# Hybrid decoder layer, one core: attention constants moved to the right of SBUF and closed with attention, and a third buffer for the raw gate and up weights

## The chip, the cores and the metric

One Trainium2 chip; the kernel runs on one of its cores. The metric is the device time of one execution in microseconds (us), as a median over runs. A core has TensorE (matrix products; PE in the profile, with its weight loads as PEld), VectorE (DVE), ScalarE (ACT), GpSimd (POOL) and SyncE, whose queue (SP) issues every DMA of this kernel. SBUF is the on-chip memory of 128 partitions, PSUM the memory that products are summed in.

## What is computed

One decoder layer on x of 1024 tokens by 1024 channels, all in float32:

```
n   = rms_norm(x)
h   = x + [ DiffAttn(n) || GLA(n) ] @ w_out
m   = rms_norm(h)
out = h + (silu(m @ w_ffn_gate) * (m @ w_ffn_up)) @ w_ffn_down
```

DiffAttn has 4 heads with two softmax maps each, GLA 4 heads of gated linear attention in chunks. The hidden width of the last line is 2816.

## The kernel before

**Precision.** Float32 products are made of three passes: each operand is cut into a high part (a cast on ScalarE, line 251) and a low part (a subtraction on VectorE, line 252), and `mm3` (lines 260 to 262) issues three matmuls per product. A cut of a weight block therefore needs the raw block in SBUF, then ScalarE, then VectorE, and only then TensorE.

**Stages.** (1) Projection of n, with both attentions woven into it by a planner (`Order`). (2) Out-projection: `po` products, h, its squares and a copy scaled by the gain (`Bf`). (3) Gate and up products, in 11 pairs (`pr` 0 to 10) of 256 hidden columns. (4) The down product.

**Gate and up.** Each pair has m = 0 (gate) and m = 1 (up). One level of a Strassen scheme makes seven products per m out of four quarters of the 1 MB raw weight block `fr`. In the trace a pair runs B11, B21, T1, T2, B22, T3, T4 (so named after the activation side), each for m = 0 and then m = 1, twelve matmuls each. The weight side is made by `a_operands` (lines 1022 to 1049): cuts a to g, of which a, b and g read the raw block, and the sums S1 to S4, made by VectorE in pair 0 and by GpSimd in all others. The high and low parts sit in rings of four (`uh`, `ul`), the sums in a ring of four (`sf`). So cut a of a pair needs the ring place of cut f of the pair before, and S1 of a pair the place of its predecessor's S4.

`load_gu(pr + 1)` stands at the top of pair `pr` and issues two loads of 1 MB, m = 0 and m = 1, into a ring of two buffers. A buffer is free again when cut g, the last reader of the raw block, is done (`ugl` in the trace).

**Activation side, pair 0 only.** `b_operands` makes T1 to T4 from h, four subtractions and four cuts each, on ScalarE and VectorE between the products. h's normalization (`rstd_begin`, `rstd_end`, lines 894 to 907) and the silu of pair 0 (`first_rest`, lines 1074 to 1090) are put into pair 0 and 1 as well.

**Order.** In this stage nothing fixes the order of an engine's instructions by hand: the framework's scheduler places each one as early as its inputs and its buffer allow, taking the one that stands first in the program where several are ready. Each engine, and the SP queue, then executes its list strictly in order. The first projection block and the end of the last pair with the down product (`tail`) keep the compute engines in program order.

**SBUF.** Pools are stacks, one from the left and one from the right. A tile in a reused place waits for the last accesses of the tiles that lay there. Left: `keep`, `const`, `small`, `ntp` (64 KB per partition: the four activation tiles, first of n, at last `mT`), `wp`, then others over it, `fl` (T2 to T4) among them; after `ntctx.close()` the pools `da` and `dw` of the down product begin behind `keep`. Right: `edge`, then `sp`, `ep`, `dp` of attention, and after `actx.close()` in their place `bp`, `fw` (with `fr`) and `fq`, and last `dl`. By the shapes, `const` and `small` take about 12.4 KB per partition, the ten `ar` buffers of `da`, into which the activations A come back, 20 KB, one `fr` buffer 8 KB.

Of the kernel before, what the change touches and what calls it, by code (L numbers as in the profile page):

```python
# [9 lines left out]
F32 = mybir.dt.float32  # L10
# [8 lines left out]
P = 128  # L19
# [3 lines left out]
ND = D // P  # L23
# [14 lines left out]
EDGE = 24  # L38
# [121 lines left out]
def decoder_layer(ctx: ExitStack, tc, xt, vecs, lams, w_proj, w_up, w_gu, w_dn, out):  # L160
    nc = tc.nc

    def pool(name, bufs=1, side="left", **k):
        return tc.tile_pool(name=name, bufs=bufs, side=side, reuse_waits="tile", **k)

    keep = ctx.enter_context(pool("keep"))
    ntctx = ExitStack()
    const = ntctx.enter_context(pool("const"))
    small = ntctx.enter_context(pool("small", 3))
    ntp = ntctx.enter_context(pool("ntp"))  # L170
    psum = ctx.enter_context(tc.tile_pool(name="psum", bufs=2, space=PSUM))
    dram = ctx.enter_context(tc.tile_pool(name="dram", bufs=1, space=DRAM))
# [14 lines left out]
    ndist = keep.tile([P, T], F32, name="ndist")  # L187


    vec = const.tile([P, 24], F32, name="vec")  # L190
    ones = const.tile([P, P], F32, name="ones")

    rsx = const.tile([P, NT], F32, name="rsx")
    nlam = const.tile([P, 1], F32, name="nlam")
# [78 lines left out]
    mixed_d = [[dram.tile([P, 512], F32, name=f"mixed{hf}_{c}") for c in range(ND)] for hf in range(2)]  # L273


    wctx, actx = ExitStack(), ExitStack()

    ctx.enter_context(pool("edge", 1, "right")).tile([P, EDGE], F32, name="edge")
    wp = wctx.enter_context(pool("wp"))
    sp = actx.enter_context(pool("sp", 1, "right"))  # L280
    ep = actx.enter_context(pool("ep", 4, "right"))
# [599 lines left out]

    def load_gu(pr):
        for m in range(2):
            raw = fw.tile([P, ND, 256], F32, name=f"fr{pr}_{m}", tag="fr", bufs=2)
            nc.sync.dma_start(raw, w_gu[pr, m].rearrange("p (d j) -> p d j", j=256))
            raws[pr, m] = raw

# [42 lines left out]
    for k, (o, n) in enumerate(OUT_COLS):  # L930
        b = NIN + k
        left = list(range(ND)) if k + 1 < len(OUT_COLS) else []
        for hf in range(2):
            if k == 0 and hf == 1:
# [4 lines left out]
                fw = fctx.enter_context(pool("fw", 1, "right"))  # L939
# [21 lines left out]
            if k == 2:  # L961
                if hf == 0:
                    load_gu(0)
                mT[hf] = new_nt(hf, "f")
                if hf == 0:
                    for c in range(ND):
                        split_b(0, c)

                    for d in range(4):
                        minus(Bf[0], Bf[2], Bf[0], d)  # L970
                    for d in range(2):
                        minus(Bf[2], Bf[3], Bf[2], d)
# [120 lines left out]
    for pr in range(NJ // 2):  # L1093
        if pr + 1 < NJ // 2:
            load_gu(pr + 1)
# [294 lines left out]
```

## Time and profile before

| | |
|---|---|
| median of 3 runs | 1244.76 us (1244.07 to 1244.89) |
| the profiled execution, its own time | 1243.45 us |
| its span, first to last instruction | 1241.7 us |
| TensorE busy | 1200.0 us, 97% |
| VectorE, ScalarE, GpSimd busy | 71%, 46%, 23% |
| mean granted TensorE clock | 0.995 |

All times below are from the span's start. A matmul's row is its modelled duration; the distance from one start to the next is what it costs when they follow each other without a gap.

### The profile page before, as it was taken

To read this page: it belongs to the slowest core of one execution; us is meant where nothing else is said; L and a number is where in the kernel's file an instruction comes from. 1 tells how busy PE (TensorE), PEld (TensorE's weight loads), DVE (VectorE), ACT (ScalarE), POOL (GpSimd) and SP (SyncE) were. 2 spreads that over 40 slices of the span, in tenths; PEclk is the share of its full clock that TensorE was granted. 3 is DMA by queue.
4 is the path that set the end of the run, shared out by engine and by line. 5 is a ranking of instruction groups with operands and counts; after the bars stand their busy time and mean duration, and the time that the engine had idled before them with its cause. 6 is when DMAs were issued, how large, how long until landed. Compare 5 with 4: busy or idle time off the path is not lost.

```text
span 1241.7 us, 17110 instructions
## 1 busy us (share of the span) xinstructions
PE 1200.0 (97%) x6068; PEld 1009.5 (81%) x6068; DVE 877.7 (71%) x1804; ACT 574.3 (46%) x1171; POOL 281.3 (23%) x282
## 2 busy tenths in 40 slices
PE   7899998999889999999989999999999999999998
PEld 7789888889878977788768788888888888888787
DVE  6765489854888777536997576866678656667885
ACT  6656354555544666635643333333333335443432
POOL 5500414000431000000053444534345330000000
PEclk9999999999999999999999999999999999999999
DMA  6101010101100623221023231322223268753351
GB/s 214 44 22 53 8 52 18 52 26 61 39 31 20 193 78 120 86 93 69 1 102 152 69 113 74 127 100 96 103 85 127 89 250 303 257 153 93 94 178 69
DMA packets 57656, 121.41 MB, mean 98 GB/s; under 512 B 5969, under 2 KB 25570, under 8 KB 53346
## 3 DMA queue, kind: packets, MB, share of 16 engines
q1 hardware_dynamic: 57570, 120.31, 28.6%
q8 instruction: 48, 0.79, 0.3%
q14 instruction: 38, 0.31, 0.1%
HBM read 88.04 MB, written 32.24 MB: 97 GB/s over the span
## 4 chain that ended last, share of the span: by engine, by line
PE 79%; DVE 11%; ACT 3%; DMA 3%; issue 2%; POOL 1%; SPq 0%; DVEq 0%; ACTq 0%; POOLq 0%
PE X L262 6%; PE X L260 6%; PE X L261 6%; PE pp L260 5%; PE pp L262 5%; PE pp L261 5%; PE s L411 3%; PE Z L262 3%; PE Z L261 3%; PE Z L260 3%; PE po L455 2%; PE po L260 2%; PE po L262 2%; PE po L261 2%; PE V L262 2%
## 5 line engine op out<-in xcount | busy, mean ns | idle before, releaser
L260 PE MATMUL pp<-wh,nh 128*128 128x384 f32 (+1 forms) x512 | 184.1, 360 | 9.4 <-ACT wh L256 7.2
L261 PE MATMUL pp<-wl,nh 128*128 128x384 f32 (+1 forms) x512 | 176.3, 344 | 0.7 <-DVE wl L257 0.7
L262 PE MATMUL pp<-wh,nl 128*128 128x384 f32 (+1 forms) x512 | 176.5, 345 | 0.0
L260 PEld LDWEIGHTS pp<-wh,nh 128*128 128x128 f32 x512 | 97.7, 191 | 18.6 <-ACT wh L256 7.2
L261 PEld LDWEIGHTS pp<-wl,nh 128*128 128x128 f32 x512 | 97.6, 191 | 2.8 <-DVE wl L257 1.8
L262 PEld LDWEIGHTS pp<-wh,nl 128*128 128x128 f32 x512 | 97.0, 189 | 3.0 <-issue 2.4
L1036 POOL TENSOR_TENSOR S1f<-fr 128x512 f32<-128x512 f32 x20 | 27.3, 1366 | 247.9 <-DVE ndist L907 238.0
L1130 POOL TENSOR_TENSOR ac<-ac,gt 128x512 f32<-128x512 f32 x30 | 46.4, 1547 | 159.8 <-DVE ac L1115 151.9
L1127 ACT ACTIVATE gt<-gt 128x512 f32<-128x512 f32 x40 | 25.3, 633 | 112.1 <-DVE gt L1126 58.8
L424 ACT ACTIVATE e<-e,nm 128x128 f32<-128x128 f32 (+7 forms) x64 | 49.3, 772 | 33.2 <-DVE nm L416 33.1
L260 PE MATMUL po<-mh,wh 128*128 128x512 f32 x128 | 51.2, 402 | 0.0
L262 PE MATMUL po<-mh,wl 128*128 128x512 f32 x128 | 50.6, 395 | 0.0
L261 PE MATMUL po<-ml,wh 128*128 128x512 f32 x128 | 50.4, 394 | 0.0
L257 DVE SCALAR_TENSOR_TENSOR wl<-wr,vec,wh 128x384 fp32r<-128x384 f32 (+1 forms) x64 | 39.5, 644 | 13.7 <-ACT wh L256 13.6
L1036 POOL TENSOR_TENSOR S4f<-fr,S2f 128x512 f32<-128x512 f32 x20 | 34.0, 1700 | 52.8 <-DVE ucl L252 52.1
L551 POOL TENSOR_TENSOR go<-go,gs 128x1024 f32<-128x1024 f32 x4 | 10.2, 2546 | 143.5 <-ACT gs L550 143.5
L1128 DVE TENSOR_TENSOR gt<-gt,ndist 128x512 f32<-128x512 f32 x40 | 31.6, 789 | 15.7 <-ACT gt L1127 14.0
L252 DVE TENSOR_TENSOR ufl<-S3f,ufh 128x512 fp32r<-128x512 f32 x22 | 15.2, 691 | 38.7 <-ACT ufh L251 38.7
L256 ACT ACTIVATE wh<-wr,vec 128x384 fp32r<-128x384 f32 (+1 forms) x64 | 37.1, 613 | 11.4 <-DMA wr<-in_w_proj 9.7
L416 DVE CUSTOM_DVE_ANT_0 e<-s,ndist 128x512 f32<-128x512 f32 (+3 forms) x64 | 36.7, 586 | 7.9 <-PE s L411 6.2
L455 PE MATMUL po<-v,wT 128*128 128x128 f32 x288 | 39.8, 283 | 1.7 <-ACT wT L445 1.7
L650 PE MATMUL pa<-Q,X 128*128 128x128 f32 x224 | 32.2, 290 | 9.3 <-POOL X L637 9.2
(555 smaller groups left out, 3539.3 us busy)
## 6 DMA issues: line engine op xcount, KB each, us to landing
fr<-in_w_gu SPq DMA_DIRECT2D x22, 1024.0 KB, 4.8
A<-act SPq DMA_DIRECT2D x77, 256.0 KB, 3.1
wr<-in_w_proj SPq DMA_DIRECT2D x72, 192.0 KB, 2.4
act<-ac SPq DMA_DIRECT2D x11, 1024.0 KB, 3.9
B<-in_w_dn SPq DMA_DIRECT2D x44, 256.0 KB, 5.4
act<-sm SPq DMA_DIRECT2D x11, 768.0 KB, 5.3
h<-in_xt SPq DMA_DIRECT2D x16, 256.0 KB, 4.9
hd<-h SPq DMA_DIRECT2D x16, 256.0 KB, 2.0
```

What stands on the lines that cost most here:

```text
L256: nc.scalar.activation(hi, src, AF.Copy, scale=gain)
L257: nc.vector.scalar_tensor_tensor(lo, src, gain, hi.bitcast(F32), ALU.mult, ALU.subtract)
L260: nc.tensor.matmul(ps, ah, bh, start=first, stop=False, **k)
L261: nc.tensor.matmul(ps, ah, bl, start=False, stop=False, **k)
L262: nc.tensor.matmul(ps, al, bh, start=False, stop=last, **k)
L411: nc.tensor.matmul(ps[m][:, :n], self.qk["q", hq][a][r, P * iq : P * iq + P], self.qk["k", ch][b][r, :n], start=(j == 0), stop=(j == 2))
L416: nc.vector.tensor_tensor_reduce(e[m][:, 512 * ch : 512 * ch + n], ps[m][:, :n], ndist[:, o : o + n], scale=-slope, scalar=nm[:, m, 0:1] i ...
L424: nc.scalar.activation(e[m][:, :cols], e[m][:, :cols], AF.Exp, bias=nm[:, m, nch - 1 : nch], scale=-1.0, accum_out=l[:, m : m + 1])
L455: nc.tensor.matmul(po[:, 0:P], self.wT[i, g][:, P * k : P * k + P], self.v[g][:, k, :], start=(kb == 0), stop=(kb == i))
L650: nc.tensor.matmul(pa[:, k], X[:, lv, :], Q[:, lv], start=True, stop=True)
L1036: (eng.tensor_sub if op == "-" else eng.tensor_add)(r, a, b)
L1130: nc.gpsimd.tensor_mul(quarter(q), quarter(q), g)
```

## The change

The constants and the small tiles go from the left stack to the right one, below the attention pools, and are closed with them; `vec` and `ones`, which later stages read, move into `keep` (`vec` is widened from 24 to 32 columns). The ring `fr` has three buffers instead of two. No arithmetic, no transfer and no line of the engines' work is added or removed.

```diff
     keep = ctx.enter_context(pool("keep"))
-    ntctx = ExitStack()
-    const = ntctx.enter_context(pool("const"))
-    small = ntctx.enter_context(pool("small", 3))
+    ntctx, wctx, actx = ExitStack(), ExitStack(), ExitStack()
+
+    ctx.enter_context(pool("edge", 1, "right")).tile([P, EDGE], F32, name="edge")
+    const = actx.enter_context(pool("const", 1, "right"))
+    small = actx.enter_context(pool("small", 3, "right"))
     ntp = ntctx.enter_context(pool("ntp"))
...
-    vec = const.tile([P, 24], F32, name="vec")
-    ones = const.tile([P, P], F32, name="ones")
+    vec = keep.tile([P, 32], F32, name="vec")
+    ones = keep.tile([P, P], F32, name="ones")
...
-    wctx, actx = ExitStack(), ExitStack()
-
-    ctx.enter_context(pool("edge", 1, "right")).tile([P, EDGE], F32, name="edge")
     wp = wctx.enter_context(pool("wp"))
     sp = actx.enter_context(pool("sp", 1, "right"))
...
-            raw = fw.tile([P, ND, 256], F32, name=f"fr{pr}_{m}", tag="fr", bufs=2)
+            raw = fw.tile([P, ND, 256], F32, name=f"fr{pr}_{m}", tag="fr", bufs=3)
```

## Rows read from the trace of the kernel before

**Rows 1.** Waits of TensorE from 600 to 1020 us: total, times, longest.
```profile
PE X L262 <- DVE ual L252: 3.5, 2, 2.0
PE X L260 <- ACT uah L251: 0.9, 1, 0.9
```

**Rows 2.** Busy time by stretch: start:end, length, each engine, granted clock, DMA.
```profile
600.00:640.00 40.00, 36.39 (x145) 27.84 (x144) 39.42 (x54) 21.08 (x35) 8.41 (x5) 0.96 0.14 53
640.00:700.00 60.00, 60.00 (x259) 48.28 (x258) 42.94 (x53) 21.49 (x38) 25.64 (x16) 1.00 0.27 99
...
636.00:638.00 2.00, 2.00 (x7) 1.52 (x6) 2.00 (x4) 0.61 (x2) 0.00 (x0) 0.50 0.00 0
```

**Rows 3.** Timeline of TensorE, pair 0 into pair 1: start, us, instruction.
```profile
621.11 0.40 PE L260 MATMUL X<-T4h,ugh 128*128 128x512 f32 x1
...
621.59 0.40 PE L262 MATMUL X<-T4h,ugl 128*128 128x512 f32 x1
...
626.47 0.39 PE L262 MATMUL X<-T4h,ugl 128*128 128x512 f32 x1
...
629.20 0.50 PE L262 MATMUL X<-fh,ual 128*128 128x512 f32 x1 [1.54 <-DVE ual L252]
...
634.25 0.50 PE L262 MATMUL X<-fh,ual 128*128 128x512 f32 x1 [2.00 <-DVE ual L252]
...
637.54 0.63 PE L260 MATMUL Y<-fh,ubh 128*128 128x512 f32 x1
...
639.39 0.40 PE L262 MATMUL Y<-fh,ubl 128*128 128x512 f32 x1
```

**Rows 4.** Timeline of the SP queue in the same stretch.
```profile
515.48 1.23 SPq L885 DMA_DIRECT2D fr<-in_w_gu  x2
...
621.37 1.62 SPq L885 DMA_DIRECT2D fr<-in_w_gu  x2
```

**Rows 5.** Timeline of ScalarE: the two cuts a of pair 1.
```profile
626.26 0.62 ACT L251 CAST uah<-fr 128x512 fp32r<-128x512 f32 x1 [1.56 <-DMA fr<-in_w_gu]
...
629.76 0.60 ACT L251 CAST uah<-fr 128x512 fp32r<-128x512 f32 x1
```

**Rows 6.** Timeline of VectorE, pair 0 into pair 1.
```profile
607.59 0.68 DVE L252 TENSOR_TENSOR uel<-S4f,ueh 128x512 fp32r<-128x512 f32 x1
...
615.81 0.69 DVE L1115 TENSOR_TENSOR ac<-Z,u 128x512 f32<-128x512 f32 x1 [0.32 <-PE Z L262]
...
620.62 0.68 DVE L252 TENSOR_TENSOR ugl<-fr,ugh 128x512 fp32r<-128x512 f32 x1
...
627.39 1.76 DVE L252 TENSOR_TENSOR ual<-fr,uah 128x512 fp32r<-128x512 f32 x1
...
632.44 1.75 DVE L252 TENSOR_TENSOR ual<-fr,uah 128x512 fp32r<-128x512 f32 x1
...
638.68 0.68 DVE L252 TENSOR_TENSOR ucl<-S1f,uch 128x512 fp32r<-128x512 f32 x1
...
652.25 1.28 DVE L252 TENSOR_TENSOR uel<-S4f,ueh 128x512 fp32r<-128x512 f32 x2
```

**Rows 7.** Timeline of GpSimd: its first sum of the stage.
```profile
626.43 2.17 POOL L1036 TENSOR_TENSOR S1f<-fr 128x512 f32<-128x512 f32 x1 [238.03 <-DVE ndist L907]
```

**Rows 8.** Costliest groups, GpSimd's S1: busy, mean ns of one, idle before.
```profile
L1036 POOL TENSOR_TENSOR S1f<-fr 128x512 f32<-128x512 f32 x20 | 27.3, 1366 | 247.9 <-DVE ndist L907 238.0
```

**Rows 9.** Timelines of ScalarE and TensorE, start of pair 3.
```profile
708.52 0.62 ACT L251 CAST uah<-fr 128x512 fp32r<-128x512 f32 x1 [1.33 <-DMA fr<-in_w_gu]
...
709.26 0.47 PE L260 MATMUL X<-T4h,ugh 128*128 128x512 f32 x1 [0.87 <-ACT uah L251]
```

**Rows 10.** Timelines of SP, TensorE and ScalarE, last pair into the down product.
```profile
996.74 0.32 SPq L1224 DMA_DIRECT2D A<-act  x1
...
1013.29 0.40 PE L260 MATMUL X<-T3h,ufh 128*128 128x512 f32 x1
...
1027.40 0.62 ACT L251 CAST da_5h<-A 128x512 fp32r<-128x512 f32 x1
```

## The prediction

> **What bounds the kernel now.** I read the page's engine totals first: TensorE is busy for 1200.0 of 1241.7 us, so only its gaps and its clock can give time back. The list of its waits says which gaps the raw gate and up weights cause: in the whole stage two waits for `ual`, the low half of cut a, 3.5 us together, and one for `uah`, its high half, 0.9 us [rows 1]. The table by stretch says where: from 600 to 640 us TensorE is busy 36.39 of 40 with a clock of 0.96, while the next 60 us are full at 1.00 [rows 2]. In those 40 us VectorE is busy for 39.42: it has nothing left to give.
>
> The timeline of TensorE gives the price of that place. A matmul follows the one before after 0.233 us (621.11 to 626.47 is 23 steps). From the last matmul of T4 at 626.47 to the first of B21 at 637.54 there are 25 steps (24 matmuls of B11 lie between), which make 5.82 us without a gap and took 11.07: 5.25 lost. From 637.54 to 639.39 five steps took 1.85 instead of 1.16: 0.69 more. Together 5.94 us [rows 3]. The two waits are 3.54 of it. Most of the other 2.4 us came behind them, when the granted clock from 636 to 638 us was 0.50, that is 1.2 in place of 2.4 GHz [rows 2]; the two gaps stand directly ahead of that fall.
>
> What ends last there: both loads of pair 1 are issued at 621.37 [rows 4], when cut g of pair 0 frees the buffer (`ugl` at 620.62, [rows 6]). The first block is there 4.9 us later, at 626.26, where ScalarE's cut has waited for the DMA [rows 5]; TensorE was through with T4 at 626.7. Then VectorE is late: `ual` starts at 627.39 and 632.44, in its strict order among the silu work of pair 0, and takes 1.76 instead of the 0.68 of `ugl`, because GpSimd's sums run beside it [rows 6, 7]. Pair 3 repeats this in small: a block comes late, TensorE idles for 0.87 us [rows 9].
>
> **The change part by part.**
>
> *The third buffer.* Pair 1's m = 0 block gets a buffer that nobody in the stage has used, so its load can follow the two of pair 0 at 515.48 [rows 4] and be done some 90 us before its use. From then on m = 0 is loaded a pair ahead, and m = 1 goes into the buffer that cut g of m = 0 frees, so it arrives when m = 0 did before. Issues and bytes are the same.
>
> Cut a of m = 0 can then be made as soon as its ring place is free, when the first half of T3 of pair 0 ends (ahead of 621.11), and stands in VectorE's list directly behind `ugl`. The block of m = 1 is there at 626.3 as before; TensorE needs its low half at the third matmul, 626.7 + 14 x 0.233 = 630.0, and VectorE reaches it at about 626.25 + 0.6 (the first `ual`) + 1.2 (one multiply) = 628.1. So both waits of [rows 1], and the clock's fall behind them, can go: 5.94, with pair 3's 0.87 a gain of 6.8 us at most.
>
> *What is late next.* VectorE: its work from 607 to 653 us is the same, and it is full. Two things eat into the gain.
>
> First, GpSimd moves. S1 of pair 1, m = 0, finds its block there and starts when its ring place is free, which is when VectorE's `uel` of pair 0 has read S4, at 608.27 [rows 6]; S2 of m = 0 follows. Before, GpSimd was idle for 238 us until 626.43 [rows 7]. Each of the two holds a VectorE subtraction up by 1.76 - 0.68 = 1.08 us [rows 6]: 2.2 us. What is queued behind them on VectorE is T3's and T4's low halves and `ugl`; for `ugl` TensorE waits, with little slack: it ends at 621.30 and its matmul starts at 621.59 [rows 3, 6]. Take off this 0.29 and the 0.32 that VectorE idled at 615.81 [rows 6]: T4 waits for 1.6 us, and the loads of `fr` behind `ugl` go out as much later. The bounds are 0, if the sums fall between two instructions, and 2.2; I take 1.6, since VectorE has no other gap there.
>
> That GpSimd and VectorE hold each other up is told by the 1.76 against 0.68. The Trainium skill says it more sharply (SBUF — State Buffer, "Who interferes with whom"): a VectorE instruction with two SBUF inputs and a GpSimd instruction that reads SBUF need the same locked port pair, and the second to come waits for the whole of the first. By that, at S1's mean of 1.37 us [rows 8], the two would cost 2.7 instead of 2.2, T4 would wait for 2.1, and the gain would be 0.5 smaller. The row decides.
>
> Second, what VectorE makes next. TensorE would be 5.94 - 1.6 = 4.3 us ahead of before, VectorE not. `ucl` was done at 639.36, its matmul came at 637.54 + 24 x 0.233 + 0.69 + 0.47 = 644.3: 4.9 us of lead, enough. `uel` was done at 652.9 [rows 6] and needed two products (48 steps) after that, at 655.5: 2.6 us of lead, 1.7 short. Bounds 0, if the scheduler puts `uel` ahead of pair 0's sums of tokens (its inputs come earlier too), and 1.7; I take 1.2, nearer to the upper end, because those sums stand first in the program.
>
> So this place gains 5.94 - 1.6 - 1.2 = 3.1 us. Pair 3 gives 0.87 more: with its two loads no longer one behind the other its block is a few us earlier.
>
> *Pairs 2 to 10.* There too S1 and S2 of m = 0 move ahead, into stretches where VectorE is busy 43 of 60 us [rows 2], and the rings of four let cuts be made several products ahead. I take 0; with that cover gone each would cost one held subtraction, 1.08 us.
>
> *The load at 517 us.* 1 MB more beside the out-projection's weights, and `fr` may start a little later, as it now lies on other attention tiles. Pair 0's products begin at 586 us (T4's start less 6 products of 5.6 and the normalization's matmuls), so 60 us cover it: 0.
>
> *The constants.* The attention stages see the same pools on fresh addresses: 0. `Bf` now lies on `const`, whose last reader is the last transpose of attention; the instructions that write `Bf` stand behind that transpose's evacuation on ScalarE: 0. At the end, `da` no longer has the 12.4 KB of `const` and `small` ahead of `mT`. Before, its 22 KB of weights and 20 KB of A ended inside the first two `mT` tiles, free after B21 of pair 10, and the first loads went out from 996.74 on. Now A buffers 5 to 9 lie on the third tile, which B22 reads until 1013.3: the load of A5 waits there, and on SP every load behind it. At the 4.9 us that 1 MB took it lands before 1018.2; its cut was at 1027.40 [rows 10]. 9 us of cover: 0.
>
> **Sum.** 3.1 + 0.9 = 4.0 us. Against the profiled execution 1243.45 - 4.0 = 1239.5 us (its span 1237.7); the median of the runs lies 1.3 above that execution, so 1240.8 us.
>
> **The rivals.** 0.2%, 2.5 us, is about what a measurement of this kernel can tell from no change.
>
> *The whole gain*, chance 0.2: the early sums fall into gaps, `uel` is made in time. 6.8 us, at least 6.3 with one short wait: 1238 to 1238.5. For it speaks that the scheduler takes each instruction as early as it can; against it the 39.42 of 40.
>
> *The wait moves*, 0.25: T4 waits 2.2 us and everything after it is paced by VectorE, whose total has not changed. What is left of the 5.94 is its 2.6 us of lead less 2.2, and pair 3's 0.87: 1.3, so 1243.5, not to be told from no change. If the third load is not issued early (the change doesn't do what it says, within the 0.25), pair 3 alone remains.
>
> *Slower*, 0.13: the gap ahead of T4 comes on top. If `ual` is still listed among the silu work, as before, T4's 2.2 us shift `ugl`, the load of m = 1 and both waits with it: 2.2 lost, 0.9 won at pair 3, and a second fall of the clock at the 2.4 us that the first cost: 1248.5. It decides once `ual` of m = 0 is not made when T4 ends.
>
> **How the numbers follow.** The forecast has 0.42, 1240.8, and its own range, 1239.5 to 1242.2, from its bounds. The range of 8 in 10 reaches down to the whole gain, 1238.0, and up past the wait that moves, 1245.2, and leaves out the slower case. Faster by over 0.2% are the forecast and the whole gain, 0.62, of which I give 0.02 to its upper edge: 0.60; within 0.2% 0.27; slower 0.13.
>
> **What would show it.** Right: a third load of `fr` near 517 us; S1 on GpSimd near 608; `ual` of m = 0 right behind `ugl`; TensorE waiting 1 to 2 us in T4 and not for `ual`; a clock of 1.00 from 626 to 642; no wait at pair 3; A5 issued when B22 ends, no cut waiting for it. Wrong: the waits for `ual` still there, a new low clock, TensorE waiting in the out-projection for weights that the early load held up, or in the down product for A.

## The result, and the profile after

The changed kernel takes 1256.13 us (median of 7 runs, 1251.66 to 1259.78), the kernel before, in runs taken beside it, 1244.89 (7 runs, 1244.07 to 1250.36): a ratio of 1.008, 95% interval 1.0062 to 1.0098. It is slower by 0.8%, some 11 us. The forecast, 1240.8 us in a range up to 1245.2, was wrong.

The profiled execution took 1259.78 us, with a span of 1258.0. Its page shows at once that no engine has more to do:

```profile
span 1258.0 us, 17115 instructions
...
PE 1208.4 (96%) x6068; PEld 1013.9 (81%) x6068; DVE 854.8 (68%) x1804; ACT 575.3 (46%) x1171; POOL 271.5 (22%) x282
```

VectorE, which was to be the limit, is busy for less time than before (68% of a longer span, against 71%). The loss is in gaps of TensorE. Its list of waits from 560 to 1060 us, the gate and up stage, answers to [rows 1]:

```profile
PE X L262 <- DVE ac L1114: 10.8, 8, 2.1
PE X L264 <- DVE ual L254: 0.7, 1, 0.7
PE Z L264 <- DVE ucl L254: 0.4, 1, 0.4
PE X L264 <- DVE ugl L254: 0.3, 1, 0.3
```

The first line is new: eight waits, 10.8 us, for an instruction that TensorE never waited for in the kernel before, `ac <- X` (line 1114 of the changed kernel, 1115 before). Here the accumulated T3 of m = 1 is read out of PSUM. T4 of m = 1 is accumulated on the same bank `X`, so its first matmul may not start before that read is done.

How much each pair lost is read from the first matmul of T4 in each pair. In the kernel before they start at 621.11, 666.23, 705.43, 745.59, 784.62, 823.66, 862.71, 901.75, 940.78, 979.83 and 1018.87 us: 39.04 a pair where nothing waits. After, they start at 627.98, 669.37, 712.35, 752.94, 793.38, 834.16, 873.36, 913.98, 954.46, 994.87 and 1035.35. This gives an account of the whole difference between the two profiled executions, 16.3 us:

| stretch | before | after | difference |
|---|---|---|---|
| start to T4 of pair 0 | 621.11 | 627.98 | +6.87 |
| T4 of pair 0 to T4 of pair 1 | 45.12 | 41.39 | -3.73 |
| T4 of pair 1 to T4 of pair 10 | 352.64 | 365.98 | +13.34 |
| T4 of pair 10 to the end | 222.8 | 222.6 | -0.2 |

**The first line belongs in the main to these two executions.** It is there before the stage begins: the two loads of `fr` that stood at 515.48 [rows 4] stand at 522.34 now, 6.86 later. Up to there VectorE, ScalarE, GpSimd and SP have the same lists of instructions in both traces, and the difference is in the clock, which in the kernel after fell, for instance, in these two stretches, where the kernel before kept 1.00:

```profile
324.00:333.00 9.00, 7.22 (x43) 7.19 (x43) 6.46 (x26) 1.31 (x2) 4.88 (x8) 0.81 0.01 2
372.00:380.00 8.00, 6.29 (x32) 6.30 (x33) 7.28 (x26) 0.43 (x2) 4.55 (x8) 0.79 0.00 0
```

(Start and end, length, busy time and instructions of TensorE, its weight loads, VectorE, ScalarE and GpSimd, granted clock, DMA share, GB/s.) The number of such falls ahead of 515 us differs from one execution to the next; the kernel with the moved pools alone (e1) has one of the two as well and takes the time of before. What sets them off stays open. The profiled execution of the changed kernel is the slowest of its seven runs, that of the kernel before is faster than all seven beside, so that the 16.3 us between them are 5 more than the 11.2 between the medians. Whether the other 2 us of this line belong to the change is not shown: T4 of pair 0 starts between 624.0 and 627.0 us in all nine experiments, later than in the one trace of the kernel before, and the fall near 326 us stands in seven of the eight traces with three buffers and in none of the three with two.

**The second line is what the change was meant to do**, 3.73 us against the 3.1 forecast. The size is less sure than it looks: with two buffers this step took 45.12 us in the kernel before and 45.13 in e6, but 43.61 in e1, so the gain lies between 2.2 and 3.7.

**The third line is the loss**, and it makes up the ratio: 13.34 - 3.73 - 0.2 = 9.4 us of some 11. Of its nine steps seven lost 1.4 to 1.7 us, one 0.2, and the first 3.9, since the clock fell behind its wait (in e2, where a wait of 2.11 us stands at this place and no fall behind it, this step takes 41.42 us in place of 42.98). The first matmuls of m = 1 of T4, with their waits, then the stretch of the fall:

```profile
674.46 0.48 PE L262 MATMUL X<-T4h,ugh 128*128 128x512 f32 x1 [2.14 <-DVE ac L1114]
...
716.61 0.47 PE L262 MATMUL X<-T4h,ugh 128*128 128x512 f32 x1 [1.31 <-DVE ac L1114]
...
757.05 0.47 PE L262 MATMUL X<-T4h,ugh 128*128 128x512 f32 x1 [1.17 <-DVE ac L1114]
...
958.53 0.48 PE L262 MATMUL X<-T4h,ugh 128*128 128x512 f32 x1 [1.11 <-DVE ac L1114]
```

```profile
674.00:678.00 4.00, 3.54 (x9) 2.88 (x10) 2.80 (x5) 0.00 (x0) 1.66 (x1) 0.60 0.01 4
```

**Why the read is late** is seen when VectorE's and GpSimd's timelines are laid side by side. First the kernel before, from pair 3 into pair 4 (VectorE, then GpSimd; start, duration):

```profile
743.70 0.68 DVE L1115 TENSOR_TENSOR gt<-X,p 128x512 f32<-128x512 f32 x1
744.41 1.23 DVE L1126 TENSOR_TENSOR gt<-gt,ndist 128x512 f32<-128x512 f32 x1
745.57 0.68 DVE L252 TENSOR_TENSOR ual<-fr,uah 128x512 fp32r<-128x512 f32 x1
746.35 0.69 DVE L1128 TENSOR_TENSOR gt<-gt,ndist 128x512 f32<-128x512 f32 x1
746.96 0.68 DVE L1115 TENSOR_TENSOR ac<-X,p 128x512 f32<-128x512 f32 x1
...
743.80 1.29 POOL L1036 TENSOR_TENSOR S1f<-fr 128x512 f32<-128x512 f32 x1 [0.75 <-DMA fr<-in_w_gu]
747.72 1.30 POOL L1130 TENSOR_TENSOR ac<-ac,gt 128x512 f32<-128x512 f32 x1 [2.62 <-DVE ac L1115]
748.97 1.29 POOL L1036 TENSOR_TENSOR S1f<-fr 128x512 f32<-128x512 f32 x1
750.22 3.44 POOL L1036 TENSOR_TENSOR S2f<-S1f,fr 128x512 f32<-128x512 f32 x2
```

Then the changed kernel, from pair 2 into pair 3:

```profile
710.46 0.68 DVE L1114 TENSOR_TENSOR gt<-X,p 128x512 f32<-128x512 f32 x1
711.06 1.40 DVE L254 TENSOR_TENSOR ual<-fr,uah 128x512 fp32r<-128x512 f32 x1
712.38 1.79 DVE L1125 TENSOR_TENSOR gt<-gt,ndist 128x512 f32<-128x512 f32 x1
714.87 1.00 DVE L1127 TENSOR_TENSOR gt<-gt,ndist 128x512 f32<-128x512 f32 x1 [0.70 <-ACT gt L1126]
715.79 0.68 DVE L1114 TENSOR_TENSOR ac<-X,p 128x512 f32<-128x512 f32 x1
...
710.62 1.29 POOL L1035 TENSOR_TENSOR S1f<-fr 128x512 f32<-128x512 f32 x1 [0.80 <-DMA fr<-in_w_gu]
711.87 3.45 POOL L1035 TENSOR_TENSOR S2f<-S1f,fr 128x512 f32<-128x512 f32 x2
716.54 1.67 POOL L1129 TENSOR_TENSOR ac<-ac,gt 128x512 f32<-128x512 f32 x1 [1.23 <-DVE ac L1114]
```

From the read of T3's m = 0 (`gt <- X`) to that of m = 1 (`ac <- X`) VectorE has a chain of cut a, two gate multiplies and between these ScalarE's silu. It took 746.96 - 743.70 = 3.26 us, and takes 715.79 - 710.46 = 5.33. The slack was small: before, that read was done at 747.64 and T4 of m = 1 began at 745.59 + 12 x 0.2325 = 748.38, so 0.74 us. 2.07 less 0.74 leaves 1.33, about the size of the waits (1.11 to 1.35 us in all but the first).

What is new beside the chain is on GpSimd. Before, one sum (S1 of m = 0) ran there; then GpSimd's own multiply of quarter 3 (`ac <- ac, gt`), which needs `ac <- X`; and behind this in its strict list the other three sums, S1 of m = 1 and S2 twice. After, S1 of m = 0 has long been made, its block being there a pair ahead; the scheduler places each instruction as early as its inputs allow, and lists these three sums *ahead* of the multiply. The one step that lost only 0.2 us fits this. There, from pair 5 into pair 6, the block of m = 1 came later, the first of the three sums began 1.4 us into the chain in place of 0.2, and the chain took 835.76 - 832.24 = 3.52 us:

```profile
832.24 0.68 DVE L1114 TENSOR_TENSOR gt<-X,p 128x512 f32<-128x512 f32 x1
...
835.76 0.68 DVE L1114 TENSOR_TENSOR ac<-X,p 128x512 f32<-128x512 f32 x1
...
833.66 1.62 POOL L1035 TENSOR_TENSOR S1f<-fr 128x512 f32<-128x512 f32 x1 [2.06 <-DMA fr<-in_w_gu]
```

Two things have changed their place at once, however: VectorE's list has `ual` of m = 0 ahead of the first gate multiply now, where it stood behind it. So three theories stood: A1, VectorE's order makes the chain longer (with `ual` ahead of the multiply, nothing covers the silu); A2, GpSimd's sums hold VectorE up; B, the tiles' new addresses cost something by themselves. The experiments take them apart.

### The profile page after: what moved, and what is told of

The parts are those of the page before. It is cut to its first block, busy times and chain, and to the rows that moved or that the text cites. A ratio compares the mean times of both kernels' runs of the same rounds, so it can differ in the third digit from the quotient of the medians.

```text
span 1258.0 us, 17115 instructions
## 1 busy us (share of the span) xinstructions
PE 1208.4 (96%) x6068; PEld 1013.9 (81%) x6068; DVE 854.8 (68%) x1804; ACT 575.3 (46%) x1171; POOL 271.5 (22%) x282
## 4 chain that ended last, share of the span: by engine, by line
PE 71%; DVE 16%; ACT 4%; issue 3%; DMA 3%; POOL 2%; SPq 0%; DVEq 0%; ACTq 0%; POOLq 0%
PE pp L262 5%; PE pp L264 5%; PE pp L263 5%; PE X L262 4%; PE X L263 4%; PE X L264 4%; PE s L410 3%; PE Z L264 2%; PE V L262 2%; PE V L263 2%; PE V L264 2%; PE po L454 2%; PE Z L263 2%; PE Z L262 2%; PE pa L649 2%
## 5 line engine op out<-in xcount | busy, mean ns | idle before, releaser
L262 PE MATMUL pp<-wh,nh 128*128 128x384 f32 (+1 forms) x512 | 186.7, 365 | 9.4 <-ACT wh L258 6.7
L1129 POOL TENSOR_TENSOR ac<-ac,gt 128x512 f32<-128x512 f32 x30 | 49.5, 1648 | 141.8 <-DVE ac L1114 133.9
L1035 POOL TENSOR_TENSOR S4f<-fr,S2f 128x512 f32<-128x512 f32 x20 | 29.7, 1484 | 76.9 <-DVE ucl L254 63.6
L262 PE MATMUL X<-T4h,ugh 128*128 128x512 f32 x88 | 35.9, 408 | 10.8 <-DVE ac L1114 10.8
L254 DVE TENSOR_TENSOR uel<-S4f,ueh 128x512 fp32r<-128x512 f32 x22 | 27.6, 1253 | 21.1 <-ACT ueh L253 21.1
```

What stands on the lines that cost most here:

```text
L262: nc.tensor.matmul(ps, ah, bh, start=first, stop=False, **k)
L1035: (eng.tensor_sub if op == "-" else eng.tensor_add)(r, a, b)
L1129: nc.gpsimd.tensor_mul(quarter(q), quarter(q), g)
```

## The experiments

The first four ran together, with the kernel before at 1244.56 us beside them (29 runs), e5 to e8 too (1245.43, 29 runs), and then e9 (1245.08, 17 runs). The lists of instructions in the traces bear the edits out on VectorE, ScalarE, GpSimd and SP: e1 has all the lists of the kernel before, e6 differs from that kernel on GpSimd alone; from the changed kernel e2 differs on VectorE alone, e3 and e7 on GpSimd alone. The third buffer without the move was not tried; what it does with the constants in their old place is not shown.

**e1, the move alone.** The constants and small tiles close with attention, `fr` keeps two buffers.

```diff
-            raw = fw.tile([P, ND, 256], F32, name=f"fr{pr}_{m}", tag="fr", bufs=3)
+            raw = fw.tile([P, ND, 256], F32, name=f"fr{pr}_{m}", tag="fr", bufs=2)
```

> The pools moved, two buffers as before. Every engine's list of instructions is the same as in the kernel before; only addresses differ. Theory A (the third buffer alone costs, through the order of work in pairs 1 to 9): the two waits for ual (3.5 us) stand again, T4 of pair 0 to T4 of pair 10 takes 397.8 us as before, no wait for ac, and the time is that of before within 0.2%. Theory B (the move itself costs, in attention, where the changed kernel's profile lost 6.9 us at a lower clock): 1248 to 1252 us with the clock low again ahead of 515 us.

1244.27 us (12 runs), ratio 0.9994, interval 0.9982 to 1.0005. The move costs nothing that can be measured, theory B falls; the loss needs the third buffer on top of the move. Not all in the trace is as expected: the two waits for `ual` are there, but 1.8 us together in place of 3.5, T4 of pair 0 to T4 of pair 10 takes 396.41 us, and pair 3 waits for nothing. A pair without a wait takes 39.20 us in this trace, and in that of e4, against 39.04 in e3, e8 and e9, so that a difference of 1 or 2 us between the stages of two traces says little.

**e2, VectorE's order set back.** All of the change, but the low half of cut a of m = 0 is issued behind the first gate multiply of quarter 3, as in the kernel before. (`issue_after` fixes the order of issue on one engine and adds no wait on another.)

```diff
                 if add is not None:
-                    nc.vector.tensor_mul(g, g, tokens(q))
+                    i = nc.vector.tensor_mul(g, g, tokens(q))
+                    if q == 3:
+                        held["gt"] = i.ins
...
-        yield cut(A11, "a")
+        with behind("gt", m == 0):
+            a = cut(A11, "a")
+        yield a
```

> The change, with VectorE's cut a of m = 0 queued behind the first multiply of quarter 3's gate, as it stood before; GpSimd's list as in the change. Theory A1 (the order of VectorE's list: the silu's 0.70 us is no longer covered by the cut): TensorE's waits for ac fall from 10.8 us to under 2, T4 to T4 of pairs 0 to 10 from 407.4 to about 396, time about 10 us below the change. Theory A2 (GpSimd's sums S1 and S2 now run beside VectorE's reads there): the waits fall only by the silu's part, to 0.6 us a pair, 5 us in all, T4 to T4 about 401, time 5 to 6 us below the change.

1258.44 us (5 runs), ratio 1.0109, interval 1.0092 to 1.0125: nothing is gained. The chain has the order of before and the length of after, 752.85 - 747.57 = 5.28 us:

```profile
747.57 0.68 DVE L1120 TENSOR_TENSOR gt<-X,p 128x512 f32<-128x512 f32 x1
748.28 1.24 DVE L1131 TENSOR_TENSOR gt<-gt,ndist 128x512 f32<-128x512 f32 x1
749.45 1.78 DVE L254 TENSOR_TENSOR ual<-fr,uah 128x512 fp32r<-128x512 f32 x1
751.16 1.77 DVE L1135 TENSOR_TENSOR gt<-gt,ndist 128x512 f32<-128x512 f32 x1
752.85 0.68 DVE L1120 TENSOR_TENSOR ac<-X,p 128x512 f32<-128x512 f32 x1
```

The 0.70 us of waiting for the silu are gone, since `ual` fills them, and yet the end is as late: three instructions that take 0.68 us alone take 1.24, 1.78 and 1.77. A1 falls. The number that A2 was given for this run, 5 to 6 us below the change, did not come either: the three sums beside the chain set its length, whatever VectorE does in the silu's time.

**e3, GpSimd's order set back.** All of the change, but S1 of m = 1 and S2 of both are issued behind GpSimd's multiply of quarter 3.

```diff
-                nc.gpsimd.tensor_mul(quarter(q), quarter(q), g)
+                i = nc.gpsimd.tensor_mul(quarter(q), quarter(q), g)
+                if q == 3:
+                    held["ac"] = i.ins
...
-        S1 = sub("+", A21, A22, "S1")
+        with behind("ac", m == 1):
+            S1 = sub("+", A21, A22, "S1")
...
-        S2 = sub("-", S1, A11, "S2")
+        with behind("ac"):
+            S2 = sub("-", S1, A11, "S2")
```

> The change, with GpSimd's S1 of m = 1 and S2 queued behind its multiply of quarter 3 of the pair before, as they stood before; VectorE's list as in the change. Theory A2 (GpSimd's sums hold VectorE up): VectorE's chain from the read of m = 0 to the read of m = 1 shrinks from 5.3 to about 3.3 us and the waits for ac go, T4 to T4 about 394, time 12 us below the change. Theory A1 (order of VectorE's list): 0.7 us a pair is left, 6 us, T4 to T4 about 400.

1241.58 us (12 runs), ratio 0.9978, interval 0.9963 to 0.9993. The loss is gone and the gain of the third buffer is left, as A2 has it. No wait for `ac` stands in the list of waits, and the chain is 748.10 - 744.91 = 3.19 us long in the very order on VectorE that the changed kernel has:

```profile
744.91 0.68 DVE L1120 TENSOR_TENSOR gt<-X,p 128x512 f32<-128x512 f32 x1
745.51 0.68 DVE L254 TENSOR_TENSOR ual<-fr,uah 128x512 fp32r<-128x512 f32 x1
746.11 0.68 DVE L1131 TENSOR_TENSOR gt<-gt,ndist 128x512 f32<-128x512 f32 x1
747.49 0.69 DVE L1133 TENSOR_TENSOR gt<-gt,ndist 128x512 f32<-128x512 f32 x1 [0.70 <-ACT gt L1132]
748.10 0.68 DVE L1120 TENSOR_TENSOR ac<-X,p 128x512 f32<-128x512 f32 x1
...
748.86 1.68 POOL L1135 TENSOR_TENSOR ac<-ac,gt 128x512 f32<-128x512 f32 x1 [4.59 <-DVE ac L1120]
750.50 1.29 POOL L1039 TENSOR_TENSOR S1f<-fr 128x512 f32<-128x512 f32 x1
751.75 1.74 POOL L1039 TENSOR_TENSOR S2f<-S1f,fr 128x512 f32<-128x512 f32 x1
```

T4 of pair 1 to T4 of pair 10 takes 351.76 us, 39.04 a pair but for one of 39.44.

**e4, both orders set back** (the edits of e2 and e3 together).

> The change with both lists set back at that place. By A1 and A2 alike no wait for ac is left, while the gain between pair 0 and 1 (3.7 us) and at pair 3 (1.1 us) stays: T4 of pair 0 to T4 of pair 10 about 393 us, time about 4 us below the kernel before, 1240 to 1241. If the waits stay, neither order is the cause.

1241.49 us (12 runs), ratio 0.998, interval 0.9969 to 0.9991. As e3: VectorE's order adds nothing.

**e5, no S2 on GpSimd.** All of the change, but in pairs 2 to 10 S2 is a plain copy of S1 made by ScalarE; the subtraction of the first quarter is left out.

```diff
-        S2 = sub("-", S1, A11, "S2")
+        if pr < 2:
+            S2 = sub("-", S1, A11, "S2")
+        else:
+            S2 = fq.tile([P, 4, P], F32, name=f"S2f{pr}_{m}", tag="sf", bufs=4)
+            nc.scalar.copy(S2, S1)
```

> The change, with S2 of pairs 2 to 10 replaced by a ScalarE copy of S1 (the subtraction of A11 is left out there, so the sums behind it hold other numbers). VectorE's list is that of the change. If GpSimd's S2 next to VectorE's reads is the cause, VectorE's chain from the read of quarter 3, m = 0, to that of m = 1 shrinks from 5.3 to about 3.9 us at most (only S1 of m = 1 is still in it) and the waits for ac go: T4 of pair 0 to T4 of pair 10 about 393 to 394 us, time as with GpSimd's list set back, 1241 to 1243. If it is something else that the third buffer brings (a DMA, ScalarE, the ring of buffers), the waits of about 1.2 us a pair stay.

1243.93 us (10 runs), ratio 0.9984, interval 0.9969 to 0.9999. Two waits for `ac` are left, 1.5 us together, in place of eight with 10.8; T4 of pair 0 to T4 of pair 10 takes 396.11 us, 2 more than expected. The longer wait, 0.81 us, comes of the edit itself: ScalarE's copy of S1 of m = 1 stands ahead of the silu and waits there for a late block, and VectorE then idles 2.37 us for the silu, ahead of 825.75.

**e6, the sums without the buffer.** The kernel of e1, two buffers, with two more GpSimd subtractions of the raw block in pairs 2 to 10 that nobody reads, listed behind S1 of m = 0 and so beside the chain. Of all lists only GpSimd's differs from that of the kernel before.

```diff
         S1 = sub("+", A21, A22, "S1")
+        if pr > 1 and m == 0:
+            for k in range(2):
+                z = fq.tile([P, 4, P], F32, name=f"z{pr}_{k}", tag="z", bufs=2)
+                nc.gpsimd.tensor_sub(z, A21, A22)
```

> Two buffers as before (pools moved), with two more GpSimd subtractions of the raw block behind S1 of m = 0 in pairs 2 to 10, whose results nobody reads. The lists of all other engines are those of the kernel before. If GpSimd beside VectorE is the whole cause, the wait for ac appears without any third buffer: the chain grows from 3.3 to about 5.3 us, against 0.75 us of slack, some 1.3 us in each of 9 pairs, time 12 us above the kernel before, 1255 to 1258. If the third buffer has to be there, the time stays near 1244.5.

1256.9 us (4 runs), ratio 1.008, interval 1.006 to 1.0101: the whole loss of the change, with two buffers and VectorE's list as it was. TensorE's waits in the stage:

```profile
PE X L262 <- DVE ac L1118: 10.2, 9, 1.3
PE X L264 <- DVE ual L254: 3.4, 2, 2.0
PE X L262 <- ACT uah L253: 0.2, 1, 0.2
```

The first line is that of the changed kernel, the second that of the kernel before [rows 1]. The two are separate things.

**e7, only S2 held.** As e3, but S1 of m = 1 is left where the scheduler puts it.

```diff
-        with behind("ac", m == 1):
-            S1 = sub("+", A21, A22, "S1")
+        S1 = sub("+", A21, A22, "S1")
```

> As the run with GpSimd's list set back, but S1 of m = 1 is left where the change has it; only S2 is held. One sum of 1.3 us is then beside VectorE's chain, as S1 of m = 0 was before. By the theory the chain takes 3.2 to 3.9 us, no more than the slack allows, and no wait for ac appears: T4 to T4 about 393 us, 1241 to 1242. If a single early sum is enough, about 0.7 us a pair is lost, 1247 to 1248.

1243.6 us (10 runs), ratio 0.998, interval 0.9967 to 0.9993. The chain is 747.14 - 743.37 = 3.77 us long, and a single wait for `ac` of 0.7 us is left in the stage, where none was expected. One sum beside the chain nearly fits into its slack, three don't.

**e8, what is left at pair 1.** As e3, and S1 and S2 of pair 1 are made by VectorE (0.6 us from start to start) in place of holding it up from GpSimd.

```diff
-            eng = nc.vector if pr == 0 else nc.gpsimd
+            eng = nc.vector if pr == 0 or (pr == 1 and nm in ("S1", "S2")) else nc.gpsimd
```

> GpSimd's list set back, and in pair 1 alone S1 and S2 are made by VectorE, at 0.6 us each, instead of by GpSimd, which holds VectorE up by 1.1 us each there. Between the T4 products of pairs 0 and 1 TensorE then loses about 1 us in place of the 2.3 (waits of 0.7 for ual, 0.4 for ucl, 0.3 for ugl and what follows them): about 1 us below that run, 1240.5. If VectorE's own work, not GpSimd, makes these waits, they stay or grow by the four sums' 2.4 us.

1243.45 us (12 runs), ratio 0.9981, interval 0.9967 to 0.9994: not told apart from e3. The waits for `ugl`, `ual` and `ucl` are gone, all three. In their place one has come, and the clock has fallen behind it:

```profile
655.27 0.50 PE L264 MATMUL Z<-fh,uel 128*128 128x512 f32 x1 [1.87 <-DVE uel L254]
```

```profile
656.00:660.00 4.00, 4.00 (x13) 3.09 (x12) 2.74 (x4) 0.76 (x2) 0.96 (x1) 0.58 0.06 25
```

Pair 0 to pair 1 takes 42.84 us, with 41.38 in e3: 3.8 us are lost there (against 39.04), where 1 was expected.

**e9, and the sums of tokens later.** As e8, with the sums of pair 0's tokens given out one product later, so that VectorE lists `uel` ahead of the last two.

```diff
-        if pr == 1:
-            next(left)
         both(Z, "B22", False, lambda m: result(m, 1, Z[m], u2[m]))
+        if pr == 1:
+            next(left)
```

> The kernel of e8 (sums of GpSimd held back in pairs 2 to 10, pair 1's S1 and S2 on VectorE) with pair 0's sums of tokens given out one product later, behind B22 of pair 1, so that VectorE lists them behind the low halves that B22 reads. In e8 those sums and GpSimd's hold `uel` up: TensorE waits 1.87 us for it at 655 us, the clock falls to 0.58 for 4 us behind it, and pair 0 to pair 1 takes 42.84 instead of 39.04 us. If the order of VectorE's list is what is late there (the forecast's step on what VectorE makes next), this wait and the fall behind it go, 0 to 1 takes 39.0 to 39.8, and the time is 2 to 4 us below e8's: 1239.5 to 1241.5. If VectorE has no room there in any order (its 39 of 40 us busy), a wait of 1 to 2 us comes back for another low half and the time is e8's, 1243.5.

1242.42 us (12 runs), ratio 0.9971, interval 0.9956 to 0.9986. The wait for `uel` is gone, but TensorE comes to T4 of pair 1 earlier than VectorE, and waits there:

```profile
667.65 0.47 PE L262 MATMUL X<-T4h,ugh 128*128 128x512 f32 x1 [1.38 <-DVE gt L1120]
```

Pair 0 to pair 1 takes 40.65 us. Against the 42.84 of e8 the order was worth 2.2 us there, and 1.6 are left that VectorE's order only pushed on. Both this and the time lie between the two that were expected. In time e3, e4 and e9 can't be told apart; all three beat the kernel before, by 0.2 to 0.3%.

## Why the prediction was wrong

**The step that failed** is the one on pairs 2 to 10: "I take 0; with that cover gone each would cost one held subtraction, 1.08 us." It looked at S1 and S2 of m = 0 and at how busy VectorE is over 60 us (43 of 60, [rows 2]), and took the idle rest for cover. A share over 60 us says nothing of one chain: the read of T3's m = 1 had 0.74 us of slack, and sums that run beside that chain cost TensorE whatever goes beyond it. VectorE is in fact less busy after the change, and its mean gate multiply of line 1125 fell (975 ns now, 1149 before); the collisions have become fewer and have moved to the one place where they count. The step also overlooked that with S1 of m = 0 out of the way, the three sums behind it need only wait for a block, and pass GpSimd's multiply. What it cost was 14.6 us in nine pairs (365.98 less 9 x 39.04), 1.6 of them by the clock that fell behind the first wait (42.98 less the 41.42 of e2), where the forecast had 0. Its other bound, 9 x 1.08 = 9.7 us, stood in the text and went into neither a rival nor the range; it would have put the time near 1250. e3 shows it by taking the sums away from that place, and e6 by putting others there without the rest of the change.

**The price of one such meeting.** The forecast took 1.08 us, from 1.76 against 0.68 [rows 6]. In the changed kernel the ends tell more: the sums end at 711.91, 713.60 (halfway through the row of two) and 715.32, the three VectorE instructions that ran beside them at 712.46, 714.17 and 715.87. Each ends 0.55 to 0.57 us behind a sum. So VectorE is not slowed by a share, it stands until the sum is over, and three sums in a row, 4.7 us, set the pace of three VectorE instructions. This is the rule that the forecast set beside the row and didn't follow, from the Trainium skill (SBUF — State Buffer, "Who interferes with whom"): the second to come waits for the whole of the first. The trace agrees with it here. By itself it would not have mended the forecast, whose step on pairs 2 to 10 counted no such meeting at all.

**The boundary of pairs 0 and 1** was right in its mechanism. That its sum came near too, 3.73 us (2.2 against e1) for 3.1, was partly luck, since the terms were not right: T4 and `uel` were to wait 1.6 and 1.2 us, and it was `ugl`, `ual` and `ucl` with 0.32, 0.72 and 0.43. The third load left early, but at 534.80 and so 12.5 us behind the other two. S1 of m = 0 of pair 1 moved to 615.28, which is 608.41 on the clock of the kernel before (less 6.87), as forecast, and `ual` of m = 0 stands at 630.01 directly behind `ugl`:

```profile
615.28 1.62 POOL L1035 TENSOR_TENSOR S1f<-fr 128x512 f32<-128x512 f32 x1 [222.89 <-DVE uel L254]
634.09 1.38 POOL L1035 TENSOR_TENSOR S1f<-fr 128x512 f32<-128x512 f32 x1 [17.18 <-DMA fr<-in_w_gu]
635.42 3.98 POOL L1035 TENSOR_TENSOR S2f<-S1f,fr 128x512 f32<-128x512 f32 x2
```

The row at 635.42 shows where the sizes went: S2 did not follow S1, so T4 waited for `ugl` 0.32 us, not 1.6; instead S1 of m = 1 and both S2 came together at 634 to 639, and `ual` of m = 1 took 1.78 us and was 0.72 late, where the forecast had it in time. `ucl`, for which 4.9 us of lead were reckoned, was 0.43 late. The clock stayed at 1.00 from 600 to 660 us, as forecast.

**What VectorE makes next**, 1.2 us for `uel`, did not show in the changed kernel, since the other three waits had used up TensorE's lead. It showed when these were gone: in e8 `uel` was 1.87 us late, behind the sums of tokens as the forecast said, and with them moved (e9) 1.4 us came back at T4.

**The load, the constants, the end.** The early load cost nothing that lasted: one wait of 0.59 us for a weight of the out-projection, at 543.86 (in small what the forecast had named as a sign of being wrong; four of the experiments with three buffers have it too, with 0.3 to 0.8 us, and no kernel with two), and pair 0 began no later for it (6.87 us behind the kernel before, with the loads of `fr` at 6.86). The move cost nothing (e1). At the end, the loads of A do wait for the last B22, though already the second load and not the sixth, and the SP queue stands from 1013.41 to 1029.97 us where before it had sent the other loads by 1010 [rows 10]:

```profile
1013.41 0.38 SPq L1215 DMA_DIRECT2D B<-in_w_dn  x1
1029.97 0.32 SPq L1223 DMA_DIRECT2D A<-act  x1
```

ScalarE's second cut waits 1.45 us for it, which the forecast had excluded; TensorE waits for the same things as before there (1.3 and 0.5 us, and before once more 0.4), and the tail is 0.2 us shorter. 0 was right. Pair 3's wait of 0.87 us [rows 9] is gone as forecast, but it is absent from e1 and e6 too, with two buffers, so it isn't shown that the third buffer took it away.

**The rivals.** The slower case had 0.13 and 1248.5 us, but for another reason, a gap ahead of T4 of pair 0; that gap was 0.32 us. None of the rivals named the chain between the two reads of T3.

## What to carry to other kernels

An earlier input re-orders more than its own reader: where a scheduler places instructions as soon as they are ready, list, for each engine, what may now pass what, and look at what runs beside it on the engine that it holds up. Cover has to be read from the chain that a late result sits in (its start, its end, and the matmul that needs it), not from the busy share of the stretch. Where GpSimd and VectorE hold each other up, queue GpSimd's free work behind the point at which VectorE's chain ends; here that turned a loss of 0.8% into a gain of 0.2%.

## What was not expected

Three GpSimd sums of 128x512 elements, one behind the other, paced VectorE: each of its two-input instructions ended 0.55 to 0.57 us behind a sum, whatever its own start, and took 1.00 to 1.79 us in place of 0.68. A wait of TensorE of 2.14 us at 674 and one of 1.87 us at 655 (e8) were each followed by a fall of the granted clock, 0.60 from 674 to 678 and 0.58 from 656 to 660 us, as the two gaps of 1.54 and 2.00 in the kernel before were [rows 2, 3], and as one of 1.35 us in e1 was, with 0.57 from 632 to 636 us. Single waits of 1.11 to 1.35 us in the changed kernel, one a pair, and three shorter ones within 22 us were not. Nor was one of 2.11 us in e2, at the place where the changed kernel's 2.14 stood:

```profile
672.52 0.47 PE L262 MATMUL X<-T4h,ugh 128*128 128x512 f32 x1 [2.11 <-DVE ac L1120]
...
672.00:676.00 4.00, 3.48 (x15) 2.89 (x16) 2.77 (x5) 0.00 (x0) 1.68 (x1) 1.00 0.02 4
```

So the length of one wait does not tell whether the clock falls behind it; what does stays open.
